# Two-operand elementwise work on VectorE alone, and a list schedule that knows a shared port

## The chip, the cores and the metric

One core of a Trainium2 chip runs the kernel, all other cores are idle. The metric is the device time of one execution in microseconds (us), as the median of several runs. Engines are called by the profile's names: PE is TensorE (matmuls), PEld its weight loads, DVE is VectorE, ACT is ScalarE, POOL is GpSimd, SP is the engine that issues most DMAs.

## The reference

One decoder layer on 1024 tokens of width 1024, in float32, for one sequence:

```python
h = rms_norm(x, norm1) * (1 + scale1) + shift1
proj = h @ w_in
q, kc_raw, vc_raw, ks, vs, kw, vw, g, cgate, bgate, u = jnp.split(proj, IN_OFFSETS, axis=-1)
...
attn_out = nsa_attention(q, kc, vc, ks, vs, kw, vw, gates, rel_bias)
z = cgate * u
...
conv_out = bgate * zc
mix = jnp.concatenate([attn_out, conv_out], axis=-1) @ w_out
x = x + gate1 * mix
h2 = rms_norm(x, norm2) * (1 + scale2) + shift2
ff = jnp.square(jax.nn.relu(h2 @ w_ff1)) @ w_ff2
return x + gate2 * ff
```

Shift, scale and gate come from a vector c through a product with `w_ada`. The attention has 8 heads of 64 and three branches (compressed keys, all causal keys, a window of 512), each with its own softmax, a bias by distance and a gate. The convolution has 3 taps. `w_ff1` is 1024 x 4096.

## The kernel before, in words

**Split operands.** Every large product is made of three matmuls (`mm3`, L443): an operand is rounded to a high part by a copy, and a low part is what the subtraction "operand minus high part" leaves. So each weight tile, each activation tile and each tile of attention probabilities costs one copy and one two-operand subtraction (`P.sub`, L333, which calls `P.tt`, L324). Weights pass through `weights` (L519, 512 columns at a time) in the first part and through `load_w` (L1250, 1024 columns) in the MLP.

**Recording and planning.** The kernel does not issue instructions directly. `Plan` (L47) records each with its memory accesses, a cost in ns and a list of engines that may take it (`alts`). `Plan.issue` (L255) makes up to eight list schedules (`_forward`, L153: whenever an engine is free, it takes the ready instruction of highest priority; `_backward`, L220, gives the priorities of the next pass), keeps the one with the shortest planned span, and issues the instructions in its order. After that the order on each engine, and which engine has which instruction, are fixed. Each engine is a resource of its own in this plan. The costs are written in the helpers: a matmul `max(0.4167 n + 2, 107)` ns for n columns (`mm`, L288), a two-operand instruction `1.04 n + 68` on DVE or `2.11 n + 148` on POOL (`tt`), a copy or an operation with constants half as long on DVE when it stays in SBUF (`copy` L313, `ts` L342).

**Choice of engine.** `EW = ("DVE", "POOL")` (L429) is the list that the two-operand calls pass: the low parts, the sums of squares (`add_square`, L511), the odd steps of `ada_cols` (L544), the products of the norms (L614, L1107), and three small steps on 128x3 tiles in each row of the attention (`row`, L917: L962 `nm`, L966 `den`, L968 `cf`). A few copies and scalings may go to ("ACT", "POOL") or to POOL alone: the high part in `weights`, the scaling of the probabilities (L970), two first steps of tables (L904).

**Stages.** There are two plans. The first holds everything up to the second norm of half 1: the adaLN products and the first norm (`ada`, L540, a DVE instruction with 1024 columns and a running sum), projections, compression, then the attention in twelve steps (`supers`, L1155), with the convolution (`conv_tile`, L1047) and, from step 4 on, the output projection, the second norm and 30 tiles of the hidden layer of half 0 (`first_half`, L1112) as filling work. In the attention a row goes from scores in PSUM through a custom DVE sum and maximum (`ttr`, L356), exponentials on ACT, small steps, scaling, and 32x32 transposes on DVE (`dvt`, L364) to DMAs that shuffle blocks (`shuffle`, L994, on SP), then to the split and the product with V. The second plan is the MLP (L1270 on).

**Queues.** DMAs go by SP, except those of queries, keys and values for the attention (L911, L912, L1183), which POOL issues.

Of the kernel before, what the change touches and what calls it, by code (L numbers as in the profile page):

```python
# [26 lines left out]
TROW = FROW + EROW  # L27
# [10 lines left out]
# ---------------------------------------------------------------- the order of the instructions  # L38
class Op:
    __slots__ = ("alts", "idx", "preds", "succs", "nbytes", "past", "end", "group")  # L40
# [6 lines left out]
class Plan:  # L47
    """Takes down instructions in program order, then issues them in the order of a list schedule.

    An instruction may be taken by any of the engines listed for it.  What depends on what follows  # L50
    from the memory that the instructions read and write.  The first schedule goes by the longest way
    to the end; the next ones by where a schedule made from the end puts the instructions.
    """

    PASSES = 8
    # from the end of an instruction to the start of one that needs it, by their engines
# [5 lines left out]
    def __init__(self, tc):  # L62
        self.tc, self.nc = tc, tc.nc
        self.eng = {"PE": self.nc.tensor, "ACT": self.nc.scalar, "DVE": self.nc.vector,
                    "POOL": self.nc.gpsimd, "SP": self.nc.sync}
        self.ops, self.mem, self.scratch = [], {}, set()
        self.group, self.ahead = "", {}  # how much earlier than its turn a group of instructions goes
        self.free = {e: 0.0 for e in self.eng}  # when the engines are through with what was issued before

    # -- recording  # L70
    @staticmethod
    def _mask(ap):
        """{group of partitions: (first column, last column + 1, columns as bits)}"""
        dims = [tuple(d) for d in ap.ap]
        off = ap.offset
        if ap.space == PSUM:  # one accumulation group at a time in a bank
            return {0: (0, 1, 1)}
        if ap.space == DRAM:
            quads, f0 = (0,), off
        else:  # L80
            ps, pn = dims[0]
            p0, f0 = divmod(off, ps)
            quads, dims = range(p0 // 32, (p0 + pn - 1) // 32 + 1), dims[1:]
        m = 1
        for s, n in sorted(dims):
            if s == 0 or n == 1:
                continue
            r, have = m, 1
            while have < n:
                k = min(have, n - have)  # L90
                r |= r << (s * k)
                have += k
            m = r
        e = (f0, f0 + m.bit_length(), m << f0)
        return {q: e for q in quads}
# [20 lines left out]
    def op(self, alts, outs, ins, nbytes=0):  # L116
        o = Op(alts, len(self.ops), nbytes)
        o.group = self.group
        for aps, wr in ((ins, False), (outs, True)):
            for ap in aps:  # L120
                if not hasattr(ap, "tensor"):
                    continue
                key = ap.tensor.name
                if ap.space == DRAM and key not in self.scratch:
                    continue
                m = self._mask(ap)
                log = self.mem.setdefault(key, [])
                for po, pm, pw in log:
                    if (wr or pw) and po is not o and self._hit(m, pm):
                        if po.end is None:  # L130
                            o.preds.add(po)
                        else:  # issued before
                            o.past.append((po, *po.end))
                if wr:
                    log[:] = [e for e in log if e[0] is o or not self._covers(m, e[1])]
                log.append((o, m, wr))
# [3 lines left out]
    # -- the schedule  # L140
# [3 lines left out]
    def _longest(self):  # L144
        """The longest way from each instruction to the end."""
# [7 lines left out]
    def _forward(self, prio):  # L153
        """[(start, instruction, choice, end)]: whenever an engine is free, the first by priority of those that are ready."""
# [5 lines left out]
        done, order, hw, dma, last, cold = bytearray(len(ops)), [], 0.0, 0.0, self.free["PE"], 0.0  # L160
# [15 lines left out]
        while len(order) < len(ops):  # L176
# [14 lines left out]
            _, idx, i = heapq.heappop(heaps[e])  # L191
            o, cost = ops[idx], ops[idx].alts[i][1]
            done[idx] = 1
            if not o.nbytes:
                if e == "PE":  # at half its rate after a rest
# [5 lines left out]
            else:  # L201
# [7 lines left out]
                if e == "SP":  # what is moved next is left open until its turn is near  # L209
# [10 lines left out]
    def _backward(self, order):  # L220
        """From the end, the last first: how long before the end each instruction starts."""
# [54 lines left out]
    # -- the instructions  # L276
# [11 lines left out]
    def mm(self, out, a, b, start, stop):  # L288
        n, m = self._n(out), self._n(a)
        c = max(0.4167 * n + 2, 107.0)  # L290
# [22 lines left out]
    def copy(self, out, a, engs=("ACT",)):  # L313
# [8 lines left out]
        self.op(alts, [out], [a])  # L322

    def tt(self, out, a, b, op, engs=("DVE",)):  # L324
# [6 lines left out]
        self.op(alts, [out], [a, b])  # L331
# [4 lines left out]
    def stt(self, out, a, s, b, op0, op1, accum=None):  # L336
# [3 lines left out]
                [out] + ([accum] if accum is not None else []), [a, b] + ([s] if ptr else []))  # L340

    def ts(self, out, a, s1, s2, op0, op1=None, engs=("DVE",)):  # L342
        n, ps, alts = self._n(out), self._ps(a, out), []
        ptr = sum(hasattr(s, "tensor") for s in (s1, s2))
        for e in engs:
# [6 lines left out]
            else:  # a product with one number for each partition  # L352
                alts.append((e, 0.833 * n + 93 + 93 * ptr, lambda: self.nc.scalar.activation(out, a, AF.Copy, scale=s1)))
        self.op(alts, [out], [a] + [s for s in (s1, s2) if hasattr(s, "tensor")])
# [25 lines left out]
class Rot:  # L380
    """A fixed set of tiles, taken in turn."""
# [9 lines left out]
class Region:  # L391
    """A stretch of columns of a tile, handed out from its left end."""
# [20 lines left out]
# columns (of 4 bytes) of the two tiles that everything of the first part lies in  # L413
# [3 lines left out]
# tiles of the hidden layer that are worked out beside the attention of half 1  # L417
# [4 lines left out]
def hymba_layer(ctx: ExitStack, tc: tile.TileContext, xT, cT, w_first, w_cols, w_vg, w_ada, w_ada2, b_ada,  # L422
# [6 lines left out]
    EW = ("DVE", "POOL")  # L429
# [18 lines left out]
    # ---------------------------------------------------------------- memory  # L448
# [47 lines left out]
    # loads on their way to be split; pieces of W_ada  # L496
# [5 lines left out]
    def rsqrt_neg2(y, t, ms):  # L502
        """y = -2 / sqrt(ms + eps): a first value from the tables, then one Newton step."""
# [7 lines left out]
    def add_square(c, sq, acc, x, engs=EW):  # L511
        """acc = the sum of the squares over the tiles of x so far"""
# [6 lines left out]
    def weights(src, rot):  # L519
        """A [128, 4, 128] piece of a weight, split in two."""  # L520
# [7 lines left out]
    # ================================================================ adaLN, first norm, projections  # L528
# [15 lines left out]
    def ada_cols(j0, n, stage, acc, bank):  # L544
        """mod of n tiles from j0 on: summed over the tiles of K, then over the partitions."""
# [33 lines left out]
    # silu(c) on every partition  # L579
# [10 lines left out]
    # a1 = -(1 + scale) * norm1 / 2  # L590
# [30 lines left out]
    # ---------------------------------------------------------------- keys, values, queries  # L621
# [56 lines left out]
    def project(c, put, hfs=(1, 0), banks=banks, rot=fw_r):  # L678
        """128 columns of the projection."""
# [9 lines left out]
    def raws(i):  # L689
        """craw[d, g, t] = raw[(g, d), t], craw[64 + d, g, t] = raw[(g, d), t + 1]"""  # L690
# [7 lines left out]
    def compress(i):  # L698
# [22 lines left out]
        # tanh-form gelu: x / (1 + exp(-2 c (x + 0.044715 x^3)))  # L721
# [59 lines left out]
    def values():  # L781
        """V and the gates, token by token; the weights by halves of K."""
# [51 lines left out]
    # rows of the bias by distance, for every head  # L834
# [25 lines left out]
    # ================================================================ attention; beside it the convolution and half of the output projection  # L860
# [8 lines left out]
    ot_r = Rot([(ot[0:64], 64), (ot[64:128], 0)])  # with the half of the sums that is copied there first  # L869
    cg_t, z_t, t1_t = ([Dr(n) for _ in range(2)] for n in (512, 514, 512))  # L870
    # keys, values, queries, split weights: for half 0, then for half 1
# [20 lines left out]
    def load_tab(hd, full, par):  # L892
        """Tables of head hd; in the first half of the tokens only the last half of them is needed."""
        tt, te, tg = tabt[hd % 2]
        d, lo = d_tab[hd], 0 if full else 512
        to = 0 if full else 512 * (par - 1)  # where column 0 would lie
# [20 lines left out]
    def row(hp, m, qp, hl, q, T0):  # L917
# [7 lines left out]
        # a bank: products (first key column, columns); sums (columns, table, place in the row, branch)  # L925
# [45 lines left out]
        # 32x32 transposes into [key in block, block of keys, half slot, (head, query in block)]  # L971
# [28 lines left out]
    def pv(hp, m, T0, o):  # L1000
# [14 lines left out]
        if ns == 2:  # two slots at a time  # L1015
# [18 lines left out]
    def products(groups, rot, h):  # L1034
        """Tiles (weight, what to do with the result); those of a group side by side."""
# [48 lines left out]
    def load_mix(hf, k, t, hi, lo):  # L1084
        """The convolution's half comes first."""
# [26 lines left out]
    def first_half():  # L1112
        """Half 0 after its attention: output projection, second norm, the first tiles of the MLP's hidden layer."""
# [85 lines left out]
    # ================================================================ half 1: output projection, second norm  # L1199
# [36 lines left out]
    # ================================================================ MLP  # L1236
# [59 lines left out]
# smallest distance of each bucket of rel_bucket()  # L1296
# [7 lines left out]
def _onehot():  # L1304
    """[33, TROW]: which bucket each distance falls in; row 32 marks a masked distance."""
# [8 lines left out]
def _cols(w):  # L1314
    """[1024, n*128] -> [n, 128, 8, 128]: column tiles, each with its eight row tiles side by side."""
# [4 lines left out]
def layout(inputs):  # L1320
# [5 lines left out]
    # the two heads of a tile of queries lie feature by feature  # L1326
# [27 lines left out]
    o["w_out"] = _cols(np.roll(a["w_out"][0], 512, 0))  # the convolution's half first  # L1354
# [20 lines left out]
```

## Time and profile before

| what | value |
|---|---|
| median of 3 runs | 1439.66 us (1437.44 to 1443.62) |
| profiled execution, its span | 1439.1 us |
| instructions in the profile | 17186 |
| busy: PE, DVE, ACT, POOL | 1293.1, 827.2, 608.0, 584.7 us |

The profiled execution has no time of its own beside its span; the span is 0.6 us below the median. "Busy" is the time in which an engine had at least one instruction running, waits inside an instruction counted. The first matmul of the MLP begins at 874.7 us, so the two plans are read as two stretches, 0 to 875 us and 875 us to the end. The granted clock of PE is given as a share of its full 2.4 GHz; its other level is 1.2 GHz.

### The profile page before, as it was taken

To read this page: it belongs to the slowest core of one execution; us is meant where nothing else is said; L and a number is where in the kernel's file an instruction comes from. 1 tells how busy PE (TensorE), PEld (TensorE's weight loads), DVE (VectorE), ACT (ScalarE), POOL (GpSimd) and SP (SyncE) were. 2 spreads that over 40 slices of the span, in tenths; PEclk is the share of its full clock that TensorE was granted. 3 is DMA by queue.
4 is the path that set the end of the run, shared out by engine and by line. 5 is a ranking of instruction groups with operands and counts; after the bars stand their busy time and mean duration, and the time that the engine had idled before them with its cause. 6 is when DMAs were issued, how large, how long until landed. Compare 5 with 4: busy or idle time off the path is not lost.

```text
span 1439.1 us, 17186 instructions
## 1 busy us (share of the span) xinstructions
PE 1293.1 (90%) x5608; PEld 1032.0 (72%) x5608; DVE 827.2 (57%) x1697; ACT 608.0 (42%) x1191; POOL 584.7 (41%) x581
## 2 busy tenths in 40 slices
PE   6689899899889888888797897989999999999998
PEld 3468688677667656666675684868888878888886
DVE  5987878789757675668784747541441252133212
ACT  5566647666536465646664434420130022103100
POOL 4733636587637574536574514111221221222120
PEclk8999999999999999989999897989999999999999
DMA  8567976887676864777769613441430232123131
GB/s 290 159 165 211 248 228 214 205 212 199 191 207 194 244 154 151 195 187 190 215 154 251 218 59 123 138 135 30 128 107 30 77 118 70 59 73 103 30 117 59
DMA packets 110029, 220.66 MB, mean 153 GB/s; under 512 B 14841, under 2 KB 40994, under 8 KB 109428
## 3 DMA queue, kind: packets, MB, share of 16 engines
q1 hardware_dynamic: 106196, 204.76, 49.5%
q0 software_dynamic: 3744, 14.81, 3.6%
q8 instruction: 44, 0.72, 0.2%
q14 instruction: 45, 0.37, 0.1%
HBM read 151.77 MB, written 36.80 MB: 131 GB/s over the span
## 4 chain that ended last, share of the span: by engine, by line
PE 49%; DVE 19%; DMA 13%; SPq 7%; issue 5%; POOL 4%; ACT 3%; DVEq 0%; POOLq 0%; ACTq 0%
PE pd L293 35%; SPq L377 7%; PE sc L293 7%; DMA FA<-FA 5%; PE fa L293 5%; DVE RA L328 5%; DVE FA L339 4%; DVE FA L365 3%; DVE FA L328 2%; POOL RA L330 2%; DMA FA<-in_w_ff 2%; DVE FA L358 2%; ACT FA L311 1%; DMA FA<-in_xT 1%; DMA FA<-in_w_ada 1%
## 5 line engine op out<-in xcount | busy, mean ns | idle before, releaser
L330 POOL TENSOR_TENSOR RA<-FA,RA 128x512 fp32r<-128x512 f32 (+4 forms) x193 | 336.5, 1752 | 521.1 <-ACT RA L317 228.2
L317 ACT CAST RA<-FA 128x512 fp32r<-128x512 f32 (+4 forms) x327 | 233.7, 736 | 587.0 <-PE pd L293 279.9
L293 PE MATMUL fa<-RA 128*128 128x512 f32 (+1 forms) x1384 | 411.6, 406 | 23.0 <-ACT FA L311 11.0
L293 PE MATMUL sc<-RA 128*128 128x512 f32 (+6 forms) x1328 | 338.1, 373 | 40.1 <-DVE mx L358 11.7
L293 PE MATMUL pd<-hid,RA 128*128 128x512 f32 x1344 | 339.5, 392 | 0.0
L293 PEld LDWEIGHTS fa<-RA 128*128 128x128 f32 (+1 forms) x1384 | 265.4, 196 | 86.7 <-ACT FA L311 14.0
L328 DVE TENSOR_TENSOR RA<-FA,RA 128x512 fp32r<-128x512 f32 (+4 forms) x214 | 215.5, 1018 | 193.2 <-PE pd L293 90.0
L293 PEld LDWEIGHTS sc<-RA 128*128 128x128 f32 x1328 | 239.5, 196 | 97.4 <-DVE mx L358 16.7
L293 PEld LDWEIGHTS pd<-hid,RA 128*128 128x128 f32 x1344 | 255.0, 190 | 53.4
L293 PE MATMUL pd<-RA 128*128 128x512 f32 x1008 | 267.9, 397 | 12.8 <-DVE RA L319 6.0
L293 PEld LDWEIGHTS pd<-RA 128*128 128x128 f32 x1008 | 191.0, 191 | 59.0 <-DVE RA L328 8.4
L339 DVE SCALAR_TENSOR_TENSOR FA<-pd,mod,FA 128x512 f32<-128x512 f32 x64 | 45.3, 746 | 219.2 <-PE pd L293 219.2
L311 ACT ACTIVATE FA<-FA,nm 128x640 f32<-128x640 f32 (+7 forms) x192 | 114.4, 597 | 42.9 <-DVE nm L347 22.0
L365 DVE STREAM_TRANSPOSE FA<-FA 128x64 f32<-128x64 f32 (+7 forms) x224 | 99.5, 482 | 41.2 <-DMA FA<-FA 23.0
L311 ACT ACTIVATE FA<-FA 128x512 f32<-128x512 f32 (+2 forms) x147 | 87.7, 616 | 25.2 <-DVE FA L339 14.6
L293 PE MATMUL stb<-RA 128*128 128x512 f32 (+1 forms) x192 | 68.5, 401 | 32.3 <-ACT RA L317 18.7
L351 POOL TENSOR_SCALAR FA<-FA,cf 128x64 f32<-128x64 f32 (+8 forms) x121 | 83.4, 701 | 21.7 <-DVE cf L328 18.3
L358 DVE CUSTOM_DVE_ANT_0 FA<-sc,FA 128x64 f32<-128x64 f32 (+5 forms) x192 | 79.9, 449 | 10.5 <-PE sc L293 10.1
L293 PE MATMUL po<-RA 128*128 128x512 f32 (+4 forms) x164 | 51.3, 380 | 21.7 <-ACT RA L317 15.9
L293 PEld LDWEIGHTS stb<-RA 128*128 128x128 f32 x192 | 36.9, 199 | 46.6 <-ACT RA L317 20.0
L321 POOL TENSOR_SCALAR RA<-FA 128x512 fp32r<-128x512 f32 x42 | 31.4, 748 | 88.2 <-DMA FA<-in_w_ff 42.8
L319 DVE CAST hid<-FA 128x512 fp32r<-128x512 f32 x56 | 42.0, 752 | 36.3 <-PE pd L293 18.8
(129 smaller groups left out, 897.6 us busy)
## 6 DMA issues: line engine op xcount, KB each, us to landing
FA<-in_w_ff SPq DMA_DIRECT2D x64, 512.0 KB, 3.6
FA<-FA SPq DMA_DIRECT2D x128, 176.0 KB, 4.0
FA<-in_w_ada SPq DMA_DIRECT2D x64, 256.0 KB, 3.9
FA<-in_w_ff SPq DMA_DIRECT2D x60, 256.0 KB, 3.8
FA<-FA SPq DMA_DIRECT2D x64, 208.0 KB, 5.2
FA<-in_w_cols SPq DMA_DIRECT2D x34, 256.0 KB, 2.9
FA<-in_xT SPq DMA_DIRECT2D x32, 256.0 KB, 4.8
FA<-in_w_ada SPq DMA_DIRECT2D x16, 512.0 KB, 3.6
```

Source lines behind the costliest of these rows:

```text
L293: self.op([("PE", c, lambda: self.nc.tensor.matmul(out, a, b, start=start, stop=stop))], [out], [a, b])
L311: self.op([("ACT", c, lambda: self.nc.scalar.activation(out, a, func, **kw))], outs, ins)
L317: alts.append((e, 0.833 * n + (53 if ps else 93), lambda: self.nc.scalar.copy(out, a)))
L319: alts.append((e, (1.04 if ps else 0.52) * n + 68, lambda: self.nc.vector.tensor_copy(out, a)))
L321: alts.append((e, 0.833 * n + 174, lambda: self.nc.gpsimd.tensor_scalar(out, a, 1.0, 0.0, ALU.mult, ALU.add)))
L328: alts.append((e, 1.04 * n + 68, lambda: self.nc.vector.tensor_tensor(out, a, b, op)))
L330: alts.append((e, 2.11 * n + 148, lambda: self.nc.gpsimd.tensor_tensor(out, a, b, op)))
L339: self.op([("DVE", 1.04 * self._n(out) + 68 + 61 * ptr, lambda: self.nc.vector.scalar_tensor_tensor(out, a, s, b, op0, op1, **kw))], [out] ...
L351: alts.append((e, 0.833 * n + 174 + 83 * ptr, lambda: self.nc.gpsimd.tensor_scalar(out, a, s1, s2, op0, op1)))
L358: self.op([("DVE", 1.04 * self._n(out) + 75, lambda: self.nc.vector.tensor_tensor_reduce(out, a, b, 1.0, init, ALU.add, ALU.max, accum))], ...
L365: self.op([("DVE", 1.04 * self._n(out) + 68, lambda: self.nc.vector.transpose(out, a))], [out], [a])
L377: self.op([(q, c, lambda: e.dma_start(out=out, in_=a))], [out], [a], nbytes=n)
```

## The change

Comments and docstrings are emptied in place, so line numbers stay the same up to the first edit. The edits that do something:

```diff
-    def op(self, alts, outs, ins, nbytes=0):
+    def op(self, alts, outs, ins, nbytes=0, port=()):
         o = Op(alts, len(self.ops), nbytes)
+        o.port = port
...
-        done, order, hw, dma, last, cold = bytearray(len(ops)), [], 0.0, 0.0, self.free["PE"], 0.0
+        done, order, hw, dma, last, cold, port = bytearray(len(ops)), [], 0.0, 0.0, self.free["PE"], 0.0, 0.0
...
-            _, idx, i = heapq.heappop(heaps[e])
+            if e in ("DVE", "POOL") and port > t:
+                h, held = heaps[e], []
+                while h and e in ops[h[0][1]].port:
+                    held.append(heapq.heappop(h))
+                    while h and done[h[0][1]]:
+                        heapq.heappop(h)
+                first = heapq.heappop(h) if h else None
+                for x in held:
+                    heapq.heappush(h, x)
+                if first is None:
+                    free[e] = min(port, pend[e][0][0]) if pend[e] and pend[e][0][0] > t else port
+                    continue
+                _, idx, i = first
+            else:
+                _, idx, i = heapq.heappop(heaps[e])
             o, cost = ops[idx], ops[idx].alts[i][1]
+            if e in o.port:
+                port = t + cost
...
-        c = max(0.4167 * n + 2, 107.0)
+        c = max(0.4375 * n + 3, 58.0)
...
-        self.op(alts, [out], [a])
+        self.op(alts, [out], [a], port=("POOL",) if ps else ("DVE", "POOL"))
...
-        self.op(alts, [out], [a, b])
+        self.op(alts, [out], [a, b], port=("POOL",) if self._ps(a, b) else ("DVE", "POOL"))
...
-                [out] + ([accum] if accum is not None else []), [a, b] + ([s] if ptr else []))
+                [out] + ([accum] if accum is not None else []), [a, b] + ([s] if ptr else []), port=() if self._ps(a, b) else ("DVE",))
...
-        self.op(alts, [out], [a] + [s for s in (s1, s2) if hasattr(s, "tensor")])
+        self.op(alts, [out], [a] + [s for s in (s1, s2) if hasattr(s, "tensor")], port=("POOL",) if ps else ("DVE", "POOL"))
...
-    EW = ("DVE", "POOL")
+    EW = ("DVE",)
```

So every call that passed `EW` now runs on DVE. In the plan, an instruction whose helper names the port for its engine is held back while the port is taken, in favour of the next that does not need it; taking it sets the port busy for the planned cost. The helpers `copy`, `tt`, `stt` and `ts` name it (for DVE only where no operand lies in PSUM); the custom sums, transposes, reciprocals, memsets and DMAs do not. The planned cost of a matmul with 512 columns goes from 215 to 227 ns. The instructions that the kernel executes stay the same in number and kind, apart from the engine and the order.

## Rows read from the trace of the kernel before

**Rows 1.** The page: its span, and busy time by engine.

```profile
span 1439.1 us, 17186 instructions
PE 1293.1 (90%) x5608; PEld 1032.0 (72%) x5608; DVE 827.2 (57%) x1697; ACT 608.0 (42%) x1191; POOL 584.7 (41%) x581
```

**Rows 2.** Stretches: busy us of PE, PEld, DVE, ACT, POOL; clock, DMA share, GB/s.

```profile
0.00:875.00 875.00, 745.00 (x3241) 584.20 (x3241) 639.57 (x1463) 495.85 (x1046) 474.89 (x532) 0.94 0.70 197
875.00:1439.00 564.00, 548.14 (x2368) 447.78 (x2368) 187.67 (x236) 112.11 (x145) 109.82 (x49) 0.98 0.28 86
...
963.00:1435.00 472.00, 469.48 (x2062) 386.56 (x2062) 132.55 (x171) 81.20 (x103) 88.78 (x38) 1.00 0.25 76
...
0.00:75.00 75.00, 48.95 (x140) 28.45 (x141) 60.18 (x91) 38.40 (x67) 48.10 (x40) 0.91 0.65 219
...
240.00:360.00 120.00, 106.50 (x507) 86.37 (x506) 103.88 (x346) 80.92 (x230) 86.71 (x142) 0.97 0.77 206
```

**Rows 3.** The chain that ended last: the whole span by engine; 875 to 1439 by line.

```profile
PE 49%; DVE 19%; DMA 13%; SPq 7%; issue 5%; POOL 4%; ACT 3%; DVEq 0%; POOLq 0%; ACTq 0%
...
by line: PE pd L293 90.0%; DVE RA L328 1.9%; DMA FA<-in_w_ada 1.4%; DVE FA L339 1.4%; DVE FA L328 1.2%; issue 1.0%; DVE hid L319 0.7%; DVE RA L319 0.5%; POOL RA L330 0.4%; ACT FA L311 0.4%; DVE hid L328 0.3%; POOL hid L330 0.2%; DVEq L328 0
```

**Rows 4.** DVE from 0 to 875 us, by form: busy us, mean ns, idle before.

```profile
L328 DVE TENSOR_TENSOR RA<-FA,RA 128x512 fp32r<-128x512 f32 x135 | 124.7, 933 | 79.8 <-ACT RA L317 39.0 <-PE sc L293 11.0 <-POOL RA L321 8.7
L328 DVE TENSOR_TENSOR RA<-FA,RA 128x1024 fp32r<-128x1024 f32 x26 | 42.7, 1652 | 14.4 <-DMA FA<-in_w_ff 9.0 <-ACT RA L317 2.9 <-PE stb L293 2.5
L339 DVE SCALAR_TENSOR_TENSOR FA<-FA 128x1024 f32<-128x1024 f32 x16 | 26.3, 1654 | 0.0
L319 DVE CAST RA<-FA 128x512 fp32r<-128x512 f32 x28 | 18.2, 652 | 8.8 <-ACT FA L311 5.9 <-DMA FA<-d_conv 2.1 <-PE stb L293 0.7
L328 DVE TENSOR_TENSOR cf<-cf,gates 128x3 f32<-128x3 f32 x37 | 16.7, 461 | 0.6
```

**Rows 5.** Tile and line views: duration ns min/median/max, first and last start.

```profile
L319 DVE CAST hid<-FA x56: 411/426/1781, 890.5 to 1351.1; 128x512 fp32r<-128x512 f32 x56
L328 DVE TENSOR_TENSOR hid<-FA,hid x51: 691/693/2834, 890.9 to 1351.5; 128x512 fp32r<-128x512 f32 x51
L330 POOL TENSOR_TENSOR hid<-FA,hid x5: 1293/1406/2059, 894.9 to 1349.2; 128x512 fp32r<-128x512 f32 x5
...
L328 DVE TENSOR_TENSOR cf<-cf,gates x37: 111/163/3423, 248.7 to 746.8; 128x3 f32<-128x3 f32 x37
...
L339 DVE SCALAR_TENSOR_TENSOR FA<-pd,mod,FA x64: 734/744/751, 955.7 to 1435.3; 128x512 f32<-128x512 f32 x64
L339 DVE SCALAR_TENSOR_TENSOR FA<-FA x31: 284/1211/2307, 19.1 to 867.6; 128x1024 f32<-128x1024 f32 x16, 128x512 f32<-128x512 f32 x14, 64x126 f32<-64x126 f32 x1
```

**Rows 6.** Timeline from 305 to 307.5 us, DVE and POOL.

```profile
305.98 1.25 DVE L347 TENSOR_SCALAR den<-den 128x3 f32<-128x3 f32 x1
...
305.48 1.73 POOL L330 TENSOR_TENSOR FA<-FA 128x512 f32<-128x512 f32 x1 [1.11 <-DVE FA L339]
```

**Rows 7.** POOL by form: three groups from 0 to 875 us, two from 0 to 75.

```profile
L330 POOL TENSOR_TENSOR RA<-FA,RA 128x512 fp32r<-128x512 f32 x109 | 160.5, 1475 | 91.1 <-PE fa L293 24.3 <-ACT RA L317 23.6 <-DVE RA L319 15.7
L330 POOL TENSOR_TENSOR RA<-FA,RA 128x1024 fp32r<-128x1024 f32 x19 | 49.2, 2592 | 25.4 <-DMA FA<-in_w_ff 9.6 <-DMA d_attn<-FA 9.4 <-ACT RA L317 6.3
L351 POOL TENSOR_SCALAR nm<-mx 128x3 f32<-128x3 f32 x38 | 16.0, 421 | 15.1 <-DVE mx L358 10.7 <-DVE cf L362 2.2 <-DVE den L347 0.3
...
L330 POOL TENSOR_TENSOR FA<-FA,FA 128x512 f32<-128x512 f32 x13 | 23.8, 1849 | 18.0 <-DVE FA L339 18.0
L330 POOL TENSOR_TENSOR RA<-FA,RA 128x512 fp32r<-128x512 f32 x7 | 14.1, 2015 | 6.9 <-ACT RA L317 4.5 <-DVE RA L319 2.3
```

**Rows 8.** POOL from 875 us on, by form.

```profile
L330 POOL TENSOR_TENSOR RA<-FA,RA 128x1024 fp32r<-128x1024 f32 x40 | 96.2, 2419 | 374.6 <-ACT RA L317 175.4 <-PE pd L293 150.8 <-ACT FA L311 31.4
```

**Rows 9.** The page's costliest groups: DVE transposes and custom sums.

```profile
L365 DVE STREAM_TRANSPOSE FA<-FA 128x64 f32<-128x64 f32 (+7 forms) x224 | 99.5, 482 | 41.2 <-DMA FA<-FA 23.0
L358 DVE CUSTOM_DVE_ANT_0 FA<-sc,FA 128x64 f32<-128x64 f32 (+5 forms) x192 | 79.9, 449 | 10.5 <-PE sc L293 10.1
```

**Rows 10.** Waits of PE from 0 to 875 us: us in total, times, longest.

```profile
PE stb L293 <- ACT RA L317: 18.7, 3, 7.2
...
PE stb L293 <- POOL RA L330: 5.4, 4, 2.0
```

More of the change, by code (lines that the diff above doesn't have):

```diff
@@ L39 @@
 class Op:
-    __slots__ = ("alts", "idx", "preds", "succs", "nbytes", "past", "end", "group")
+    __slots__ = ("alts", "idx", "preds", "succs", "nbytes", "past", "end", "group", "port")
     def __init__(self, alts, idx, nbytes):
```

## The prediction

> **What bounds the kernel now.** I read the page first: PE is busy for 90% of the span, DVE for 57%, POOL for 41% [rows 1]. These shares average two stages, so the next view is the busy time by stretches [rows 2]. From 875 us on PE works 548 of 564 us, and from 963 to 1435 us 469 of 472 us at full clock: 2062 matmuls in 472 us, 229 ns each. The chain of waits says the same: 90% of that stretch is PE [rows 3]. Nothing that DVE or POOL do there can be worth more than the 16 us in which PE rests.
>
> Up to 875 us no engine is full: PE 745 us busy, DVE 640, ACT 496, POOL 475, DMA share 0.70, granted clock 0.94 [rows 2]. PE rests 130 us, and a mean of 0.94 between its two levels (1.2 and 2.4 GHz) means 12% of the stretch, 105 us, at the lower. Whatever the change gives or takes comes from here. The chain splits by engine into DVE 19%, DMA 13%, SP's queue 7%, POOL 4% [rows 3]. Of DVE's 19% (273 us) the MLP holds 6.0% of 564 us, 34 us, so 239 us lie in the first stretch: 37% of DVE's busy time there. Of POOL's 4% (58 us) the MLP holds 3, which leaves 55.
>
> The third view is DVE by form. Before 875 us a subtraction of 128x512 takes 933 ns on average and a cast of that size 652 [rows 4]; in the tile view the medians are 693 and 426, the minima 691 and 411, the longest 2834 and 1781 [rows 5]. So the short value is the price of the work, and the rest is a wait inside the instruction. The timeline shows with whom: a 128x3 step takes 1.25 us while POOL is inside a two-operand instruction of 1.73 us [rows 6]. The accumulations that read PSUM never stretch (734 to 751 ns) [rows 5]. DVE and POOL delay each other, and only where DVE works in SBUF alone. That is the list which the edited plan is given.
>
> **The change part by part.**
>
> *What leaves POOL.* In the first stretch 145 two-operand instructions of 128x512 (the 109 shown and two groups of 21 and 15), 19 of 128x1024, some 20 of other widths, and 97 small steps (38 shown, then 32 and 27) [rows 7]. Their busy time, summed over these groups, is 332 of POOL's 475 us, 70%.
>
> *What comes to DVE.* 145 x 0.69 us = 100; 19 x 1.21 us (the 1024-wide form nearest to it, median 1211 ns) = 23; the other widths by the same slope 11; 97 x 0.16 = 16 [rows 5]. Sum 150 us. Since neighbours on DVE overlap by some 0.08 us, 130 is the lower end.
>
> *What DVE no longer waits for.* Mean minus undisturbed price: 135 x (0.933 - 0.692) = 32.5; 26 x (1.652 - 1.211) = 11.5; 16 x (1.654 - 1.211) = 7.1; 28 x (0.652 - 0.426) = 6.3; 37 x (0.461 - 0.163) = 11.0 [rows 4, 5]. That is 68 us; some ten further groups of this pattern give about 50 by the same subtraction. Sum 120 if nothing collides any more. POOL keeps 143 us of scalings and copies, so half, 60, is the lower end. I take 120, since the plan now keeps the two apart and 70% of POOL's work is gone. DVE's load thus hardly moves: +150 - 120.
>
> *On the chain.* From 18 to 75 us DVE never rests (60 of 75 us [rows 2]), so all counts. POOL's two-operand work there, 20 of 512 columns [rows 7] and 6 of 384, costs DVE 17 us; the waits removed from the `ada` instructions and their neighbours are 25 of the 120. Net -8. In the rest DVE's chain share is (239 - 50) of (640 - 60) us, 33%: added 133, removed 95, net +38 x 0.33 = +13. POOL's own steps on the chain lose their 70%: -38. Their work is already counted on DVE. Sum -33.
>
> *Clock.* PE's rests shrink by about a quarter (33 of 130). The lower level costs 105/2 = 52 us of full-speed time; a quarter of it is 13, and I take less than half, -5, since the first 20 us of cold start stay.
>
> *The order.* The new matmul cost, 227 ns, is nearer than 215 to the 229 measured [rows 2]; it costs nothing itself, but both plans come out in another order. No row prices this. I bound it by +10 (one rest of PE of the longer kind, 7.2 us [rows 10], and its slow clock) and -20 (a sixth of the 130 us), and take 0, the nearest to a plan whose waits I have already counted.
>
> *Queues.* No DMA is added. POOL's 26 issues stand behind less work; SP's order follows the plan. I take nothing for either, since the transfers stay as long as they are; if SP comes to issue the shuffles later, each late one costs what PE then waits, inside the +10 above.
>
> *The MLP.* 40 subtractions of 1024 columns [rows 8] go to DVE: 40 x 1.21 = 48 us, plus 9 smaller ones, 6 us, on an engine busy 188 of 564 us. PE's back-to-back matmuls cover this. Without that cover it would cost 54 us.
>
> Sum: -33 - 5 = -38 against the profiled span of 1439.1, which lies 0.6 us below the median of the runs: 1401. After that, DMA landings and the ACT casts behind them are late next. Ends: with DVE's overlap used and the better order, -4 in all more at the start, +6 instead of +13, clock -10, order -20: -74, 1365. With half the waits left and a worse order: start +5, rest +28, POOL -38, clock 0, order +10: +5, 1444.
>
> **Rivals.** About 0.5%, 7 us, is what a measurement of this kernel can tell from no change.
>
> *The port as the bound.* DVE's busy time less transposes, custom sums and their reads, 640 - 100 - 80 - 20 = 440 us [rows 2, 9], plus POOL's 475 is 915 us in a stretch of 875. If the two exclude each other and this pair sets the pace, the change cuts the sum to 440 + 150 - 120 + 143 = 613, and the stretch shrinks until PE, 745 us busy, is next: some 790 us with its cold start, a gain of 85, total 1354. Against it: POOL ends few of PE's waits, the largest entry being 5.4 us [rows 10], and 20% of the chain is transfers and their issue. The Trainium skill's page SBUF — State Buffer, section on the two sides of SBUF, calls the pair an exclusive lock held for a whole instruction, the loser blocked; by it the time would be this 1354, and the trace agrees where a 128x3 step took 1.25 us [rows 6]. Chance 0.10.
>
> *DVE becomes the bound: slower.* From 240 to 360 us DVE is busy 104 of 120 us, POOL 87 [rows 2]. If POOL's remaining scalings disturb DVE as much as before, nothing is removed: start +17, rest 133 x 0.33 = +44, POOL -38, total +23, 1462. It decides from the point where less than three tenths of the 120 us is removed (23 - 56 x 0.29 = +7); then DVE's queue also delays the 97 small steps on which exponentials wait. For it: it gives up an engine that did 332 us of work in parallel. Against it: the transposes and sums do not stretch, and the alternatives price at half. The Trainium skill's page Perfetto Trace Analysis, section Optimizing Scalar/DVE Operations, advises handing work to GpSimd when DVE is saturated, and doubts it because of the shared port; the first half of that advice gives this rival's time, but here DVE is 73% busy, not saturated. Chance 0.14.
>
> *Nothing moves.* Transfers and their issue hold 20% of the chain, and PE's longest waits end on ACT (18.7 us [rows 10]), behind a DMA. If every shortened DVE step only uncovers one of these, the time stays within 7 us, 1439. Chance 0.13.
>
> *The plan does not do what it says.* Planned and real times drift apart, so instructions planned side by side still meet. Half of the 120 stays: start +5, rest +28, POOL -38, clock -2: -7, 1432, on the edge between faster and same. Chance 0.08.
>
> **How the numbers follow.** Forecast 0.55, port 0.10, DVE-bound 0.14, unmoved 0.13, drift 0.08. Faster: 0.55 + 0.10 + half of 0.08 = 0.69, and the rest of the drift case falls to same, 0.17; slower 0.14. The range 1365 to 1444 holds the forecast's ends, the unmoved and the drift case; left out are the port (0.10) and most of the slower one.
>
> **What would show it.** Right: DVE's 128x512 subtractions near 0.70 us instead of 0.93 and casts near 0.43; 128x3 steps without values of 3 us; POOL busy near 145 us before the MLP, DVE still near 640 to 670; the `ada` products ending near 67 instead of 75 us; the first matmul of the MLP near 837 us; the MLP itself within 3 us. Wrong: subtractions still above 0.85 us (the port is not relieved); DVE above 90% busy in the attention with PE waiting for it (the slower rival); or all of this as forecast and the MLP starting within 7 us of 875, with PE's waits ending on ACT and DMA (unmoved).

## The result and the profile after

The changed kernel takes 1396.6 us as the median of 4 runs (1390.8 to 1400.0), the kernel before 1439.9 (1437.4 to 1443.6) beside it. The ratio is 0.9695 with a 95% interval of 0.9666 to 0.9725: 43 us or 3.0% faster. The forecast was 1401 in a range of 1365 to 1444. In the profiled executions the span goes from 1439.1 to 1396.7 us. The first matmul of the MLP begins at 844.2 instead of 874.7 us, which is 30.5 us of the gain; the MLP takes 552.5 instead of 564.4 us, which is 11.9. Lines of `kernel.py` from `_forward` on are 17 higher than before: `tt` on DVE is L345, `copy` L334 to L338, `stt` L356.

The page of the changed kernel: span, busy time by engine, the chain by engine.

```profile
span 1396.7 us, 17048 instructions
PE 1278.2 (92%) x5608; PEld 1031.4 (74%) x5608; DVE 835.7 (60%) x2019; ACT 619.0 (44%) x1206; POOL 131.2 (9%) x244
...
PE 59%; DMA 14%; DVE 13%; SPq 7%; ACT 4%; issue 3%; POOL 0%; DVEq 0%; ACTq 0%; POOLq 0%
```

POOL does 131 us of work where it did 585 [rows 1], and DVE, which took over 322 more instructions, is busy 836 us instead of 827. The work that came in and the waits that went out cancel, as the forecast had it.

The stretches (columns as in [rows 2]), now cut at 844 us:

```profile
0.00:844.00 844.00, 738.36 (x3240) 587.77 (x3240) 636.15 (x1733) 503.88 (x1055) 131.16 (x244) 0.93 0.72 202
844.00:1396.00 552.00, 539.88 (x2368) 443.64 (x2368) 199.60 (x287) 115.15 (x153) 0.00 (x0) 0.99 0.29 90
...
0.00:75.00 75.00, 58.97 (x189) 37.45 (x189) 58.43 (x135) 49.34 (x84) 1.88 (x16) 0.91 0.70 238
...
240.00:360.00 120.00, 101.26 (x453) 82.25 (x452) 93.66 (x349) 65.18 (x183) 25.79 (x54) 0.90 0.77 197
```

DVE by form from 0 to 844 us, the same forms as in [rows 4]:

```profile
L345 DVE TENSOR_TENSOR RA<-FA,RA 128x512 fp32r<-128x512 f32 x242 | 163.7, 691 | 60.5 <-ACT RA L334 24.4 <-PE sc L310 13.8 <-DMA FA<-in_w_out 6.6
L345 DVE TENSOR_TENSOR RA<-FA,RA 128x1024 fp32r<-128x1024 f32 x45 | 54.5, 1224 | 17.7 <-DMA d_attn<-FA 16.2 <-PE po L310 1.5
L356 DVE SCALAR_TENSOR_TENSOR FA<-FA 128x1024 f32<-128x1024 f32 x16 | 19.1, 1220 | 3.2 <-ACT FA L334 3.2
L345 DVE TENSOR_TENSOR cf<-cf,gates 128x3 f32<-128x3 f32 x64 | 11.1, 186 | 0.2
L336 DVE CAST RA<-FA 128x512 fp32r<-128x512 f32 x21 | 9.5, 451 | 1.3 <-PE stb L310 1.2
```

And the tile and line views that answer to [rows 5]: duration in ns min/median/max, first and last start.

```profile
L336 DVE CAST hid<-FA x56: 415/421/428, 858.9 to 1309.0; 128x512 fp32r<-128x512 f32 x56
L345 DVE TENSOR_TENSOR hid<-FA,hid x56: 680/685/694, 859.3 to 1310.0; 128x512 fp32r<-128x512 f32 x56
...
L345 DVE TENSOR_TENSOR cf<-cf,gates x64: 114/154/574, 228.2 to 738.1; 128x3 f32<-128x3 f32 x64
```

Here one sees the collisions end. The mean of the 128x512 subtraction, 933 ns before, is now 691, within 2 ns of the old median; the longest cast of the hidden layer is 428 ns where it was 1781, the longest 128x3 step 574 where it was 3423. A count of the single instructions in the two traces says with whom they collided. Before, VectorE has 196 such subtractions in the whole span. The 96 that share no time with any GpSimd instruction took 644 to 695 ns. All 48 that took more than 700 ns share time with GpSimd arithmetic: 38 with a two-operand instruction (of 68 that do so), 10 with one that has a single tensor operand, such as a scaling (of 30). In the changed kernel 10 of 314 took more than 700 ns, up to 1096, each beside a scaling or copy.

The chain from 844 us to the end, by line, and the waits of PE over the whole span (us in total, times, longest):

```profile
by line: PE pd L310 93.4%; DMA FA<-in_w_ada 2.0%; ACT FA L328 1.6%; DVE FA L345 0.8%; ACT RA L334 0.5%; issue 0.4%; DVE FA L356 0.3%; DVE RA L345 0.2%; DVE hid L336 0.1%; DVE hid L345 0.1%; DVEq L345 0.0%; SPq L394 0.0%
```

```profile
PE po L310 <- ACT RA L334: 26.8, 6, 8.9
PE stb L310 <- ACT RA L334: 20.1, 3, 11.2
PE sc L310 <- DVE mx L375: 8.9, 2, 5.1
```

What PE now waits for longest is the same as before [rows 10]: ACT's casts of the attention probabilities, which stand behind the shuffling DMAs. (`sc`, `po` and `stb` are PSUM tiles: in the attention `sc` holds scores, and `po` and `stb` the products with V; `fa` has the filling work and `pd` the MLP.) In the longest of these waits, 11.2 us, SP issues sixteen shuffles in a row, and then ACT casts:

```profile
746.24 15.88 SPq L394 DMA_DIRECT2D FA<-FA  x16
...
767.63 3.98 ACT L334 CAST RA<-FA 128x1024 fp32r<-128x1024 f32 x5 [8.80 <-DMA FA<-in_w_ff]
```

The last of the sixteen lands at 767.45 us in the trace, just before the cast, although the view names another DMA as what ended ACT's wait.

### The profile page after: what moved, and what is told of

Its sections match the earlier page's. It is cut to its first block, busy times and chain, and to the rows that moved or that the text cites. A ratio compares the mean times of both kernels' runs of the same rounds, so it can differ in the third digit from the quotient of the medians.

```text
span 1396.7 us, 17048 instructions
## 1 busy us (share of the span) xinstructions
PE 1278.2 (92%) x5608; PEld 1031.4 (74%) x5608; DVE 835.7 (60%) x2019; ACT 619.0 (44%) x1206; POOL 131.2 (9%) x244
## 4 chain that ended last, share of the span: by engine, by line
PE 59%; DMA 14%; DVE 13%; SPq 7%; ACT 4%; issue 3%; POOL 0%; DVEq 0%; ACTq 0%; POOLq 0%
PE pd L310 37%; PE fa L310 10%; PE sc L310 9%; SPq L394 7%; DMA FA<-FA 5%; DVE RA L345 3%; DVE FA L382 3%; ACT FA L328 2%; PE stb L310 2%; DVE FA L356 2%; DVE FA L345 2%; DMA d_x<-FA 2%; DVE FA L375 1%; ACT RA L334 1%; PE po L310 1%
## 5 line engine op out<-in xcount | busy, mean ns | idle before, releaser
L334 ACT CAST RA<-FA 128x512 fp32r<-128x512 f32 (+4 forms) x323 | 231.5, 738 | 585.6 <-PE pd L310 286.3
L345 DVE TENSOR_TENSOR RA<-FA,RA 128x512 fp32r<-128x512 f32 (+5 forms) x407 | 319.7, 809 | 185.1 <-PE pd L310 95.0
L310 PE MATMUL fa<-RA 128*128 128x512 f32 (+1 forms) x1384 | 398.9, 407 | 18.2 <-DVE RA L345 8.0
L310 PE MATMUL sc<-RA 128*128 128x512 f32 (+6 forms) x1328 | 319.0, 368 | 22.5 <-DVE mx L375 8.9
L310 PEld LDWEIGHTS sc<-RA 128*128 128x128 f32 x1328 | 236.3, 194 | 70.9 <-DVE mx L375 12.1
L310 PE MATMUL pd<-RA 128*128 128x512 f32 x1008 | 263.9, 393 | 8.6 <-ACT RA L334 6.0
L356 DVE SCALAR_TENSOR_TENSOR FA<-pd,mod,FA 128x512 f32<-128x512 f32 x64 | 46.1, 745 | 201.1 <-PE pd L310 201.1
L382 DVE STREAM_TRANSPOSE FA<-FA 128x128 f32<-128x128 f32 (+8 forms) x224 | 97.4, 481 | 60.3 <-DMA FA<-FA 53.6
L328 ACT ACTIVATE FA<-FA,nm 128x64 f32<-128x64 f32 (+6 forms) x192 | 114.1, 596 | 23.2 <-DVE nm L364 21.2
L368 POOL TENSOR_SCALAR FA<-FA,cf 128x64 f32<-128x64 f32 (+8 forms) x107 | 68.5, 654 | 109.2 <-DVE cf L345 89.6
L338 POOL TENSOR_SCALAR RA<-FA 128x512 fp32r<-128x512 f32 x54 | 35.2, 654 | 276.2 <-DMA FA<-in_w_ff 78.6
L310 PEld LDWEIGHTS po<-RA 128*128 128x128 f32 (+1 forms) x164 | 30.7, 206 | 38.5 <-ACT RA L334 30.1
L370 ACT ACTIVATE FA<-FA,cf 128x64 f32<-128x64 f32 (+8 forms) x85 | 50.1, 633 | 11.3 <-DVE cf L345 8.5
```

The costliest lines, as they stand in the source:

```text
L310: self.op([("PE", c, lambda: self.nc.tensor.matmul(out, a, b, start=start, stop=stop))], [out], [a, b])
L328: self.op([("ACT", c, lambda: self.nc.scalar.activation(out, a, func, **kw))], outs, ins)
L334: alts.append((e, 0.833 * n + (53 if ps else 93), lambda: self.nc.scalar.copy(out, a)))
L338: alts.append((e, 0.833 * n + 174, lambda: self.nc.gpsimd.tensor_scalar(out, a, 1.0, 0.0, ALU.mult, ALU.add)))
L345: alts.append((e, 1.04 * n + 68, lambda: self.nc.vector.tensor_tensor(out, a, b, op)))
L356: self.op([("DVE", 1.04 * self._n(out) + 68 + 61 * ptr, lambda: self.nc.vector.scalar_tensor_tensor(out, a, s, b, op0, op1, **kw))], [out] ...
```

## The experiments

The change has three parts that do something: the **engine list** (two-operand work on VectorE alone), the **port** in the plan, and the **matmul cost** of the plan. The first eight runs, with the two kernels, make all eight combinations of them and two controls; the last four follow up what those showed. Each time is a median of at least four runs, beside runs of the kernel before (medians 1439.8 to 1441.9 us).

**One part at a time.** The engine list alone, on the kernel before:

```diff
-    EW = ("DVE", "POOL")
+    EW = ("DVE",)
```

> The kernel before with only the engine list changed: all two-operand work on VectorE; the list schedule knows no port and keeps the old matmul cost (215 ns). If the gain of 43 us comes from collisions between the two engines that end with the move (theory), most of it is here: 1400 to 1412 us, subtractions of 128x512 near 0.70 to 0.73 us. If it comes from the better informed order (rival), this run stays within 8 us of the kernel before, 1432 to 1448.

Measured 1399.0 us, ratio 0.9727 (0.9706 to 0.9749): 41 us faster. The subtractions are at their price without any help of the plan. From 0 to 851 us:

```profile
L345 DVE TENSOR_TENSOR RA<-FA,RA 128x512 fp32r<-128x512 f32 x242 | 164.6, 696 | 56.9 <-ACT RA L334 19.1 <-PE sc L310 14.9 <-DMA d_attn<-FA 9.2
```

The port alone: the changed kernel with both engines in the list and the old matmul cost.

```diff
-    EW = ("DVE",)
+    EW = ("DVE", "POOL")
-        c = max(0.4375 * n + 3, 58.0)
+        c = max(0.4167 * n + 2, 107.0)
```

> The kernel before with only the port made known to the list schedule: two-operand work may still go to GpSimd, matmul cost 215 ns. Theory: GpSimd takes less, since the plan sees that it blocks VectorE, but where it does take a subtraction it holds the port 1.3 us for what VectorE does in 0.7, so a third to a half of the gain: 1418 to 1430 us. Rival (order is what counts): at least as good as the changed kernel, 1390 to 1402.

Measured 1379.7 us, ratio 0.9589 (0.9560 to 0.9618). The theory fell here: I had expected 1418 to 1430, and it is faster than the full change. GpSimd keeps 76 of its 109 subtractions of 512 columns, and yet disturbs far less. From 0 to 830 us, where the MLP begins in this run:

```profile
L347 POOL TENSOR_TENSOR RA<-FA,RA 128x512 fp32r<-128x512 f32 x76 | 102.0, 1346 | 123.3 <-ACT RA L334 69.2 <-DMA FA<-in_w_out 11.1 <-PE fa L310 10.0
...
L345 DVE TENSOR_TENSOR RA<-FA,RA 128x512 fp32r<-128x512 f32 x166 | 119.1, 736 | 56.3 <-ACT RA L334 30.9 <-PE sc L310 8.9 <-PE fa L310 7.2
...
L345 DVE TENSOR_TENSOR RA<-FA,RA 128x1024 fp32r<-128x1024 f32 x23 | 34.1, 1492 | 13.4 <-DMA FA<-in_w_ff 9.8 <-ACT RA L334 2.3 <-PE stb L310 1.4
```

The mean on DVE is 736 ns (933 before [rows 4]), on POOL 1346 (1475 before [rows 7]); the 1024-wide form still stretches most, 1492 against 1652. By its rule the plan, in its own times, lets POOL's subtractions run only beside work of DVE that needs no port. So collisions can be ended in two ways, by taking the work away from POOL or by keeping the two apart.

The matmul cost alone, on the kernel before:

```diff
-        c = max(0.4167 * n + 2, 107.0)
+        c = max(0.4375 * n + 3, 58.0)
```

> The kernel before with only the planned matmul cost changed (227 instead of 215 ns for 512 columns, 58 instead of 107 as the floor). Theory: another order, the same collisions, 1432 to 1447 us. Rival (a truer plan of TensorE's time brings the gain): under 1425.

Measured 1465.2 us, ratio 1.0181 (1.0153 to 1.0209). Neither expectation held: the truer cost makes the kernel 25 us slower. The collisions are the same; before the MLP a subtraction takes

```profile
L345 DVE TENSOR_TENSOR RA<-FA,RA 128x512 fp32r<-128x512 f32 x135 | 127.2, 948 | 66.2 <-ACT RA L334 38.0 <-PE sc L310 11.4 <-PE fa L310 7.2
```

**Order held, collisions taken away.** The plan of the kernel before with its costs and order, but two-operand tensor_tensor instructions planned for POOL are issued on DVE. The 70 steps `nm` and `den`, which are of another kind, stay where the plan put them.

```diff
-                alts.append((e, 2.11 * n + 148, lambda: self.nc.gpsimd.tensor_tensor(out, a, b, op)))
+                alts.append((e, 2.11 * n + 148, lambda: self.nc.vector.tensor_tensor(out, a, b, op)))
```

> The plan of the kernel before is kept as it is, with its order and its times; only at issue the two-operand tensor_tensor instructions that it gave to GpSimd go to VectorE instead, in the order of their planned starts. So the order is the old one and the collisions of these instructions are gone. Theory: most of the gain, 1402 to 1420 us, a little short of the changed kernel because the plan does not know how full VectorE is. Rival (order is what counts): 1440 or worse, up to 1465, since VectorE gets 150 us more work in an order made for two engines.

Measured 1410.9 us, ratio 0.9816 (0.9785 to 0.9847): 29 us faster in an order that was made for two engines. From 0 to 852 us, those planned for DVE and those moved to it:

```profile
L345 DVE TENSOR_TENSOR RA<-FA,RA 128x512 fp32r<-128x512 f32 x134 | 94.9, 716 | 60.7 <-ACT RA L334 23.2 <-PE sc L310 10.9 <-PE po L310 8.2
L347 DVE TENSOR_TENSOR RA<-FA,RA 128x512 fp32r<-128x512 f32 x109 | 75.3, 691 | 5.6 <-ACT RA L334 3.4 <-PE po L310 1.2 <-POOL RA L338 0.8
```

This run separates the move from the order: the same plan, the same instructions, only the engine is another. It shows that moving these instructions is worth 29 us in the old order; 12 more come when the plan knows where they run and `nm` and `den` move too (1399.0). It does not separate the two things that the move brings: the collisions end, and a moved subtraction itself takes 691 ns where GpSimd took 1475 [rows 7]. The run with the port alone shows that the second is not needed for a gain, since most of the subtractions stay on GpSimd there, at 1346 ns; but its order is another, so how the 29 us split is not shown.

**The other combinations.** The changed kernel without the port, `o.port = ()` in place of `o.port = port`:

> The changed kernel without the port in the plan: two-operand work on VectorE alone, matmul cost 227 ns. Theory (the move ends nearly all collisions, so the plan's knowledge has little left to do): 1396 to 1408 us, as for the engine list alone, 1399. Rival (knowing the port is worth as much beside the move as it is without it, 60 us): 1440 or more. A third reading, that the new matmul cost costs about 25 us wherever it is used: about 1424.

The changed kernel with the old matmul cost, as in the diff of the port alone:

> The changed kernel with the old matmul cost (215 ns): VectorE alone, port known. Theory: 1390 to 1403 us, not different from the changed kernel by more than orders differ by chance. If the new matmul cost is bad by itself (25 us, as where it was changed alone): about 1372.

The changed kernel with both engines in the list:

> The changed kernel with both engines in the list again: port known, matmul cost 227 ns. If moving all two-operand work to VectorE gives away what GpSimd can do beside VectorE's transposes and PSUM reads (theory after the first runs), this is faster than the changed kernel: 1372 to 1386 us. If the port alone was quick by a lucky order (rival): 1396 us or more.

And a setting that has nothing to do with the change, on the kernel before:

```diff
-AHEAD = {"pv5": 100}
+AHEAD = {}
```

> The kernel before with one setting changed that has nothing to do with engines, port or costs: the group of the sixth step's products with V is no longer taken 100 ns ahead of its turn. It shows how far an unrelated new order alone moves the time. Theory: collisions stay, so 1425 to 1455 us; anything outside that would say that one run of each variant can't tell a cause of 20 us from the order.

The last one gives 1442.9 us, ratio 1.0008 (0.9985 to 1.0031): that new order moves nothing, though it is a single one. The others gave 1408.7 (0.9742 to 0.9809), 1389.7 (0.9606 to 0.9684) and 1394.2 (0.9630 to 0.9721). The first and second lie just outside the theory's ranges, 0.7 us above and 0.3 us below; the third, expected at 1372 to 1386 or from 1396 on, fell between the two. All eight, in us:

```text
                         matmul cost 215 ns    matmul cost 227 ns
both engines, no port         1439.9                1465.2
both engines, port            1379.7                1394.2
VectorE alone, no port        1399.0                1408.7
VectorE alone, port           1389.7                1396.6  (the change)
```

Read by rows: without the port in the plan, the move gains 41 or 57 us; with it, nothing (+10 and +2). Without the move, the port gains 60 or 71 us; with it, 9 or 12. They are two ways to the same thing, and who has one needs little of the other. Read by columns: the truer matmul cost loses 25, 15, 10 and 7 us, four times with the same sign. (The 7 us in the change's own row, the 10 us in the row above it, and the 10 between one engine and two are differences of ratios whose intervals touch, measured on different chips; the sign of all four together is the stronger evidence.) The 25 us that I had thought possible wherever the cost is used are there only where collisions remain.

**Why is the truer cost worse?** Its two halves apart, then a value further from the truth, all with the port known and both engines in the list:

```diff
+        c = max(0.4375 * n + 3, 107.0)     (slope)
+        c = max(0.4167 * n + 2, 58.0)      (floor)
+        c = max(0.38 * n + 2, 107.0)       (quicker)
```

> Port known, both engines in the list (1380 us with the old matmul cost, 1394 with the new). Of the new cost only the slope: 0.4375 n + 3, with the old floor of 107 ns. If the loss of 14 us comes from a slower TensorE in the plan (theory: a plan in which TensorE looks like the bound takes the feeding of it less seriously), this run is near 1394, 1388 to 1400. If it comes from the floor (rival: score matmuls and others of few columns look too cheap): near 1380, 1374 to 1386.

> The same with only the floor changed: 0.4167 n + 2 with a floor of 58 ns. Theory (slope): near 1380, 1374 to 1386. Rival (floor): near 1394, 1388 to 1400. If neither this run nor the one with the slope alone lies clearly at one of the two, the loss is the accident of an order.

> The same with a matmul cost further below what TensorE needs: 0.38 n + 2, 197 ns for 512 columns, floor 107. If a plan with a quicker TensorE is the better one (theory of the slope), this is at or below 1380: 1362 to 1380 us. If the truer cost is only unlucky (rival), there is no direction: 1380 to 1400.

And the unrelated setting once more, `AHEAD = {}` on the kernel with the port alone:

> Port known, both engines, old matmul cost (1380 us), and the group of the sixth step's products with V no longer taken 100 ns ahead. A second look at how far an unrelated order moves the time, in the quicker family: 1375 to 1386 us if as little as in the kernel before (+1 us); 1390 or more would put the differences of 7 to 15 us between variants within what an order does by chance.

Measured: slope 1393.1 (ratio 0.9637 to 0.9706), floor 1378.6 (0.9521 to 0.9632), quicker 1362.1 (0.9431 to 0.9495), unrelated setting 1379.3 (0.9534 to 0.9628), against 1379.7 with the old cost. So the floor does nothing, the one unrelated order nothing, and the slope decides: 1393 or 1394 at 0.4375, 1379 or 1380 at 0.4167, 1362 at 0.38. The third is the best kernel of the study, 78 us (5.4%) under the kernel before and 34 under the change.

Where this time lies can be read from the first stretch up to the MLP and from PE's waits, for the slope run, the run with the port alone, and the quicker one:

```profile
0.00:841.00 841.00, 729.79 (x3241) 580.98 (x3241) 584.15 (x1513) 517.03 (x1086) 326.84 (x434) 0.94 0.72 205
...
PE po L310 <- ACT RA L334: 32.3, 6, 7.5
PE stb L310 <- ACT RA L334: 18.1, 3, 8.4
PE sc L310 <- ACT RA L334: 14.8, 5, 11.2
```

```profile
0.00:830.00 830.00, 731.77 (x3241) 584.62 (x3241) 582.24 (x1516) 516.66 (x1089) 329.01 (x428) 0.94 0.73 207
...
PE po L310 <- ACT RA L334: 23.7, 5, 8.0
PE stb L310 <- ACT RA L334: 21.3, 3, 10.2
PE sc L310 <- ACT RA L334: 10.2, 1, 10.2
```

```profile
0.00:816.00 816.00, 732.45 (x3241) 582.95 (x3241) 583.73 (x1513) 516.02 (x1089) 337.33 (x438) 0.95 0.75 213
...
PE po L310 <- ACT RA L334: 14.0, 5, 4.4
PE sc L310 <- ACT RA L334: 13.6, 3, 11.5
...
PE stb L310 <- ACT RA L334: 5.6, 1, 5.6
```

The work is the same to some 10 us on every engine; PE's rest shrinks from 111 to 98 to 84 us, and these three waits for ACT's casts from 65 to 55 to 33. The longest `sc` wait (11.2, 10.2 and 11.5 us) lies before 75 us in all three, ahead of the attention; `po` and `stb` together go from 50 to 45 to 20, and 3 of the 45 lie before the attention. So from the second run to the third, what the plan with a quicker TensorE does better is to have the attention's casts ready in time; from the first to the second these casts explain some 8 of the 13 us, and the rest stays open. That the plan does so because it ranks what feeds TensorE higher when TensorE itself looks cheap is my reading of how the list schedule sets priorities; no run shows it.

## Why the prediction was right, and where its steps were not

**The waits that end: right.** I took all of some 120 us as removed, against 60 as the lower end. The means of the five forms in [rows 4] fell to within 25 ns of their undisturbed price, and the DVE of the first stretch is busy 636 us where the text expected 640 to 670. The order-held run and the engine list alone show that the move by itself brings the gain, without the new costs and, in the first of them, without a new order.

**POOL: right.** 131 us against some 145 expected.

**The start: right.** I expected a gain of 8 us up to 75 us from cheaper steps. By then PE has done 189 matmuls instead of 140 [rows 2]; at 229 ns each that is 11 us. The last running sum of the `ada` products is read at 54 instead of 72 us, not at 67, and the same later step of DVE (`kns`, 128x1) comes at 64.0 instead of 74.5 us. That DVE is as busy as before (58 of 75 us) doesn't speak against cheaper steps: it did 135 instructions in that time, not 91. Nor is it the new order. The run with the order held, and the run with another order but the collisions kept, show in the same 75 us:

```profile
0.00:75.00 75.00, 58.65 (x185) 36.44 (x186) 58.20 (x134) 46.17 (x81) 1.88 (x16) 0.93 0.70 237
```

```profile
0.00:75.00 75.00, 49.94 (x139) 28.32 (x140) 60.45 (x90) 36.67 (x63) 49.74 (x40) 0.91 0.75 237
```

The first has 185 matmuls with the old order, the second 139 with a new one.

**The sum on the chain: right in total, wrong in its terms.** The step that failed is the chain's share, "added 133, removed 95, net +38 x 0.33 = +13": it took the share of DVE's busy time on the chain as fixed. By the chain, DVE in the first stretch went from 239 to about 173 us (13% of 1396.7 less 1.5% of 552), POOL from 55 to 0, together -121. What came late next is PE itself: its part of the first stretch's chain went from about 197 us (49% of 1439 less 90% of 564) to 308. DMA stayed (179 to 184). (The shares are printed in whole per cent, so each of these is good to some 7 us.) I had expected DMA and ACT to take the place; instead the chain ran over PE. That the moved work on DVE fell into gaps is how I read this; no run shows it by itself. The stretch gave 30.5 us where the sum said 38, and the MLP 11.9 where it said nothing: that the total came within 5 us of the forecast is in part luck, since these two errors cancel.

**The clock: wrong.** I put down -5. The granted clock of the first stretch is 0.93, not above 0.94, so about 118 us at the lower of its two levels against 105. PE rests less in sum (106 against 130 us), but more from 240 to 360 us, in the attention: 19 us against 13.5, at a granted clock of 0.90 against 0.97, and it does 453 matmuls there instead of 507. (The window holds other work than before: by 240 us the changed kernel is 982 matmuls far, not 892.) The "first 20 us of cold start" that I kept out of the term are not in the trace either: from 10 to 25 us the granted clock before is 1.00.

**The MLP: wrong.** I put it at nothing, "within 3 us"; it gave 11.9. The cover I named, back-to-back matmuls, begins only at 963 us. In the 89 us before that, PE did 306 matmuls; in the same 89 us of the changed kernel it did 344, with a higher clock.

```profile
874.00:963.00 89.00, 78.65 (x306) 61.49 (x306) 55.21 (x66) 31.03 (x43) 21.43 (x12) 0.88 0.44 136
```

```profile
844.00:933.00 89.00, 79.99 (x344) 65.13 (x345) 50.11 (x79) 35.25 (x50) 0.00 (x0) 0.94 0.50 157
```

That is 38 x 0.229 = 8.7 us. The bound that I named, the 16 us in which PE rests, was not passed, but it isn't one: it took PE's busy time as fixed. Of the 11.9 us only some 4 are rest (15.9 to 12.1 us, by the stretches [rows 2] and above); 8.3 are busy time, since the same 2368 matmuls took 539.9 instead of 548.1 us at a granted clock of 0.99 instead of 0.98. The runs agree that this goes with the collisions: the MLP takes 562 to 565 us in the three kernels whose two engines collide as before, and 543 to 555 in the eleven others, whichever part ended or thinned the collisions.

**Queues: nearly.** The shuffles' median time from issue to landing went from 4.0 to 4.9 us in one of their two groups and from 5.2 to 4.7 in the other (the pages' list of DMA issues); the DMA on the chain stayed.

**The order: too small.** I took 0 between +10 and -20. In the change the new matmul cost loses some 7 us, so without that part it would have been 1389.7; and the matmul cost alone, through the order, reaches from 1465 to 1440 without the port in the plan and from 1394 to 1362 with it, both engines in the list. The argument that 227 ns is better because it is nearer to the measured 229 was wrong: nearer was slower each time.

**The rivals.** The port as the bound came nearest to the mechanism but not to the time: freed of the port, the stretch stops at 844 us, not 790: PE works 738 us of it, and the longest of its waits are those for casts shown above. The Trainium skill's page SBUF — State Buffer, section on its two sides, has the pair as an exclusive lock, held for a whole instruction. The trace agrees in [rows 6]: the 128x3 step ends at 307.23 us, 0.02 us after GpSimd's instruction (307.21). And the 933 ns became 688 to 716 in each of the runs without GpSimd's two-operand tensor work. DVE as the bound did not come: it is busy 94 of 120 us in the stretch that the rival named, less than the 104 before. What the text beside it said of transposes and custom sums holds: their means stayed at 482 and 449 ns [rows 9] to within 1 ns, though GpSimd's load fell to less than a quarter.

```profile
L382 DVE STREAM_TRANSPOSE FA<-FA 128x128 f32<-128x128 f32 (+8 forms) x224 | 97.4, 481 | 60.3 <-DMA FA<-FA 53.6
...
L375 DVE CUSTOM_DVE_ANT_0 FA<-sc,FA 128x64 f32<-128x64 f32 (+5 forms) x192 | 80.3, 450 | 6.1 <-PE sc L310 5.4
```

The advice in the Trainium skill's page Perfetto Trace Analysis, section Optimizing Scalar/DVE Operations, is that offloading between these two engines might not help because of the port. The runs agree where the plan doesn't know the port: GpSimd's help costs 41 or 57 us there. With the port known to the plan, its help is worth 10 us or 2, little more than these runs can tell from nothing. "Unmoved" and "drift" are refuted by the interval and by the 691 ns.

## What to carry to other kernels

Where the mean of an instruction is well above its minimum, and each long one has one other engine busy inside it, suspect that the two share something: either give the work to one of them, or tell the planner, which did here at least as well and keeps the second engine. A cost in a list schedule is a knob before it is a measurement: a truer one lost time in four of four pairs, so sweep it on the chip. When one resource is freed, don't scale its share of the chain; ask which engine the chain will run over instead.

## What was not expected of the hardware

Some 131 us of GpSimd work remain, most of it scalings and copies in SBUF, and 165 us in the run with the engine list alone; yet VectorE's subtractions there are at 691 and 696 ns on average. These scalings do still disturb: of the 128x512 subtractions that share time with one, 10 of 35 took more than 700 ns in the changed kernel, and 16 of 50, up to 1400, with the engine list alone, where the plan knows no port. They are too few, among 314, to move the mean much. And the granted clock did not rise with fewer rests: 0.93 against 0.94 in the first stretch, with PE resting 106 us against 130.
